# Macaron transformer layer: the additions to x of the last product but one, held behind the fifth chunk's operands in both feed-forwards

## The chip, the cores and the metric

The kernel runs on one core of a Trainium2 chip. The metric is the device time of one execution in microseconds (us). Five engines work in parallel and each takes its instructions strictly in the order of its queue: TensorE (PE, matrix products), VectorE (DVE, element-wise work), ScalarE (ACT, element-wise functions and copies), GpSimd (POOL, element-wise work here) and SyncE (SP, which issues the DMAs). An instruction that waits for another engine holds up everything behind it on its own engine.

## The reference

One layer on x of 1024 rows by 1024 columns: a feed-forward, a causal attention, a feed-forward.

```
x = x + 0.5 * swiglu(rms_norm(x, g1), w1_in, w1_out)
x = x + stick_breaking_attention(rms_norm(x, gm), w_qkv, gq, gk, w_o)
x = x + 0.5 * swiglu(rms_norm(x, g2), w2_in, w2_out)

def swiglu(xn, w_in, w_out):                 # w_in 1024 x 5632, w_out 2816 x 1024
    gate, up = split(xn @ w_in, 2)
    return (silu(gate) * up) @ w_out
```

All is float32. The edit is in the second matrix product of each feed-forward, `@ w_out`, and in the addition of its result to x.

## The kernel before, in words

**Products of three.** Each float32 operand is split in a high part and a low rest (function `split`, lines 182 and 183: ACT copies the high part, DVE or POOL subtracts it from the operand to get the low part). Each product is three matmuls (function `mm3`): high by high (line 279), high of the hidden values by low of the weights (line 280), low of the hidden values by high of the weights (line 281).

**The second product of a feed-forward** (function `ffn_out`) is done in blocks of 2 x 2 by Strassen's way: seven products instead of eight, numbered m = 1 to 7 and taken in the order 5, 1, 4, 3, 7, 2, 6 of the table `SEVEN`. Each product's operands are mixtures of blocks of the weights (mixed by DVE, line 524) and mixtures of blocks of the hidden values, which the feed-forward's first half left in DRAM. The inner length of each product comes in six chunks (numbered 0 to 5 in the code): five of two pieces and a sixth of one. For each chunk `operands` loads, mixes and splits: the hidden part's low half goes to DVE, but for chunks 1, 3 and 5 of product 6 to POOL; the weights' low half always goes to POOL. Each product sums up in four PSUM banks of 128 x 512, tags "ma" or "mb". The last product but one, m = 2, lies in the four "mb" banks, the last, m = 6, in the four "ma" banks.

The last product takes its first three chunks for all four banks (24 matmuls each), and then, bank by bank ("block 0" to "block 3"), the last three chunks (15 matmuls each), so that results come out one after another.

**Additions to x.** A finished bank is added to one or two quarters of x, which is in SBUF as two halves of 512 columns, tiles x0 and x1 (function `result`, line 570, DVE). Product 2 goes to both halves: eight additions of 128 x 512, two for each of its four banks. Product 6 goes to x1 alone: four additions, one behind each block.

**Holding.** `ffn_out` takes `held`. With `held=None` the eight additions of product 2 follow it at once in program order. With a number they are left until the last product's operands have been written down, and made to depend on chunk `held` of them:

```
there = ops[held][1][1][:, 0, 0:1].bitcast(F32)
signs = cpool.tile([P, 2], F32, name="signs")
dve.tensor_scalar(signs, there.to_broadcast([P, 2]), 1.0, None, op0=ALU.mult)
late_result(signs, ops)
```

`ops[held][1][1]` is the low half of that chunk's hidden operand. `signs` reads it (line 576), is then overwritten by two memsets with the factors +0.5 and -0.5 (line 536), and the additions take their factor from it. So none of them can start before that low half is there. The scheduler, which orders the instructions of each engine, sets the rest.

**What follows in the first feed-forward.** The hook `at` does, for product 2's half of x: squares of x0 with their sums (line 217, ACT, tile `hs`) and stores of x0 to `x_keep` (line 672, SP). For rows 6 and 7 of eight, whose x was ready earlier, it makes the normalised rows `xs` on DVE (line 242; the one-column writes of line 240 hold them behind the third chunk's low half). PE transposes them (line 254) into the "mb" banks behind block 0 of product 6, ACT and DVE split them into `xh` and `xl`. For the rows whose x is ready last DVE takes squares' sums to rates (lines 191 to 198) and normalises each block. The attention's first projection (`bq`, its weights `wqh` and `wql`) follows; its weights come by SP (`raw_qkv`, line 733) and are split by ACT (line 739) and POOL (line 742).

**In the second feed-forward** the hook only stores the output (line 1104, SP).

Before, the first feed-forward has `held=2`, the third chunk; the second has no `held`.

Of the kernel before, what the change touches and what calls it, by code (L numbers as in the profile page):

```python
# [9 lines left out]
F32 = mybir.dt.float32  # L10
# [7 lines left out]
P = 128  # L18
# [88 lines left out]
def macaron_kernel(ctx, tc, x, g1, w1_in, w1_out, gm, w_qkv, gq, gk, w_o, g2, w2_in, w2_out, out):  # L107
# [3 lines left out]
    cpool = ctx.enter_context(tc.tile_pool(name="cpool", bufs=1))  # L111
# [8 lines left out]
    @contextmanager  # L120
    def pools(*names, side=None):

        with ExitStack() as s:
            yield {n: s.enter_context(tc.tile_pool(name=n, bufs=2, side=side, reuse_waits="tile")) for n in names}
# [3 lines left out]
    @contextmanager  # L128
    def banks(name):

        with tc.tile_pool(name=name, bufs=1, space=PSUM, reuse_waits="tile") as p:
            psum.append((p, {}))
            yield
            psum.pop()
# [37 lines left out]
    make_identity(nc, ident)  # L172
    xh = cpool.tile([P, KD, T], F32R, name="xh")
    xl = cpool.tile([P, KD, T], F32R, name="xl")
    above = cpool.tile([P, 96], F32, name="above")
    pool_e.memset(below, 0.0)
    pool_e.memset(above, 0.0)
    x_keep = [dram.tile([T, D], F32, name=f"x_keep{i}") for i in range(2)]
# [22 lines left out]
    def load_gain(pl, g):  # L201

        t = pl["xs"].tile([P, D], F32, name="gain", bufs=1)
        sp.dma_start(t, g.broadcast_to([P, D]))
        return t
# [3 lines left out]
    def rows(tb):  # L209
        return slice(tb * P, (tb + 1) * P)  # L210
# [18 lines left out]
    def norm(pl, row, tbs, gain, ss=None, r=None, behind=None):  # L229

        if r is None:
            r = rates(pl, row, tbs, ss)
        turns = []
        for i, tb in enumerate(tbs):
            xs = pl["xs"].tile([P, D], F32, name="xs")
            if behind is not None:
                dve.tensor_scalar(xs[:, 0:1], behind, 1.0, None, op0=ALU.mult)  # L240
            for h in range(2):
                dve.scalar_tensor_tensor(
                    out=xs[:, HALVES[h]], in0=row(tb, h), scalar=r[:, i : i + 1], in1=gain[:, HALVES[h]],
                    op0=ALU.mult, op1=ALU.mult,
                )
            turns.append(partial(turned, xs, tb))
        return turns
# [35 lines left out]
    def mixed(pl):  # L283

        return [pl[f"tl{i}"].tile([P, 4, NHALF], F32, name=f"tl{i}", bufs=1) for i in range(4)]
# [10 lines left out]
    def stream(pl, w_in, q, part):  # L296

        c0 = part * F + q * 2 * P
        halves = []
        for d in range(2):  # L300
            raw = raw_tile(pl).rearrange("p (k c) -> p k c", k=4)
            sp.dma_start(
                raw, w_in[d * NHALF : (d + 1) * NHALF, c0 : c0 + 2 * P].rearrange("(k p) c -> p k c", p=P)
            )
            halves.append(raw)
        return halves
# [286 lines left out]
    def keeps(name):  # L593

        return {
            m: [dram.tile([P, len(qs), NHALF], F32, name=f"{name}_{m}_{c}") for c, qs in enumerate(CHUNKS)]
            for m in range(1, 8)
        }
# [17 lines left out]
    keep = keeps("k1")  # L616
    pending = []
    with pools(*RAWS) as pr:
        ops = {}
        right = ExitStack()  # L620
        tl = mixed(right.enter_context(pools(*MIXED, side="right")))
        with banks("ps1"), pools(*STREAM) as pa:
            with pools("x") as px, pools("xs", "hs", side="right") as pl:
                rows_of = {}

                def load_x(tbs):
                    for tb in tbs:
                        rows_of[tb] = px["x"].tile([P, D], F32, name="x", bufs=NT)
                        sp.dma_start(rows_of[tb], x[rows(tb), :])

                def normed(tbs):
                    pending.extend(norm(pl, lambda tb, h: rows_of[tb][:, HALVES[h]], tbs, gain))

                def turn_rows(tbs):
                    while pending:
                        pending.pop(0)("kb", tl)
                    if tbs:
                        normed(tbs)

                load_x(ORDER[:2])  # L640
                gain = load_gain(pl, g1)
                ahead = [stream(pr, w1_in, 0, 0)]
                load_x(ORDER[2:4])
                ahead.append(stream(pr, w1_in, 0, 1))
                load_x(ORDER[4:])
                for tb in ORDER[:2]:
                    normed((tb,))

                us = first_weights(pa | pr, ahead, pending[1].args[0][:, D - 1 :])
                turn_rows(ORDER[2:4])  # L650
                at = {(0, 3): 4, (1, 1): 6, (2, 1): 8}
                hb = first_pair(
                    pa | pr, us, {w: lambda i=i: turn_rows(ORDER[i : i + 2]) for w, i in at.items()}
                )
            with pools(*SPLIT) as pt:
                ffn_in(pa | pr | pt, w1_in, keep, tl, hb, right, lambda: early(pr, w1_out, keep, ops))
        late = []
        norms = ExitStack()
        pn = norms.enter_context(pools("xs", "hs", side="right"))
        with banks("ps2"), pools(*SECOND) as pl:  # L660
            lay_banks()
            gain_m = load_gain(pn, gm)
            half = pn["xs"].tile([P, 4, 2], F32, name="half", bufs=1)

            def at(x_sb, m, where, ops):
                def row(tb, h):
                    return x_sb[h][:, tb, :]

                def store(tbs, hs):
                    for tb in tbs:  # L670
                        for h in hs:
                            sp.dma_start(x_keep[0][rows(tb), HALVES[h]], row(tb, h))

                def turn_rows(bk, n):
                    for _ in range(n):
                        pending.pop(0)(bk)

                if (m, where) == (7, "end"):
                    pending.extend(norm(pn, row, (4, 5), gain_m))
                    store((4, 5, 6, 7), (0, 1))  # L680
                elif (m, where) == (2, 2):
                    turn_rows("ma", 2)
                elif (m, where) == (2, 3):
                    late.append(rates(pn, row, (6, 7)))
                elif (m, where) == (6, 0):

                    there = ops[2][1][1][:, 0, 0:1].bitcast(F32)
                    pending.extend(norm(pn, row, (6, 7), gain_m, r=late.pop(), behind=there))
                elif (m, where) == (2, "end"):
                    squares(pn, row, range(4), half, (0,))  # L690
                    store(range(4), (0,))
                elif m == 6 and str(where).startswith("block"):
                    t = int(where[-1])
                    turn_rows("mb", (2, 0, 0, 1)[t])
                    squares(pn, row, (t,), half[:, t : t + 1], (1,))
                    late.append(lambda: pending.extend(norm(pn, row, (t,), gain_m, half[:, t : t + 1])))
                    if t < 3:
                        late.pop()()
                    store((t,), (1,))

            ffn_out(pl | pr, w1_out, keep, x, ops, at, held=2)

    on_banks = ExitStack()
    on_banks.enter_context(banks("psa"))
# [3 lines left out]
    with ExitStack() as stack:  # L708
        pl = dict(stack.enter_context(pools(
            "raw_qkv", "wq1", "wq0", "wq2", "wq3", "vst0", "qk1", "qk0", "vst1", "st1", "st0", "sq",  # L710
        )))
# [247 lines left out]
        for p in range(-1, NP):  # L959
# [32 lines left out]
            if 0 <= p < NP - 2:  # L992

                held = (
                    ((dve, 0, lambda s=nxt: s["r"][:, 0, 0:1]), (pool_e, 1, lambda s=nxt: s["qk", 1][:, 0, 4, 0:1])),
                    ((pool_e, 0, lambda s=nxt: s["qk", 0][:, 2, 0, 0:1]),),
                )
# [21 lines left out]
    keep = keeps("k2")  # L1019
    after = ExitStack()  # L1020
    pr = after.enter_context(pools(*RAWS))
    pn = norms.enter_context(pools("xs", "hs", side="right"))
    with pools(*PROJECTION) as pl:
        pl = pl | pr | pn
# [60 lines left out]
    ops = {}  # L1085
# [5 lines left out]
    with banks("ps4"), pools(*SECOND) as pl:  # L1091
        lay_banks()

        def at(x_sb, m, where, ops):
            tbs, hs = (), ()
            if (m, where) == (7, "end"):
                tbs, hs = (4, 5, 6, 7), (0, 1)
            elif (m, where) == (2, "end"):
                tbs, hs = range(4), (0,)
            elif m == 6 and str(where).startswith("block"):  # L1100
                tbs, hs = (int(where[-1]),), (1,)
            for tb in tbs:
                for h in hs:
                    sp.dma_start(out[rows(tb), HALVES[h]], x_sb[h][:, tb, :])

        ffn_out(pl | pr, w2_out, keep, x_keep[1], ops, at)
    after.close()


# [37 lines left out]
```

## Time and profile before

| | |
|---|---|
| Runs | 1952.72 us median of 3 (1952.14 to 1958.2) |
| Profiled execution | 1957.07 us, its span 1955.3 us |
| PE busy | 1910.4 us, 98% of the span |
| DVE, ACT, POOL busy | 1265.6, 986.2, 1089.5 us |
| Mean granted clock of PE | 0.999 |
| End of the first feed-forward's last product | about 672 us |
| Last product of the second feed-forward | about 1916 to 1951.5 us |

A row of a timeline gives the start in us, the duration in us, engine, line and operation, what is written and read, a count, and in brackets how long the engine sat idle before and what released it. The matmuls of the profile overlap: one of 0.39 us starts every 0.227 us. `x`, `ma` or `raw` in the profile stand for all tiles of the name; the order's rows below have them with numbers.

### The profile page before, as it was taken

To read this page: it belongs to the slowest core of one execution; us is meant where nothing else is said; L and a number is where in the kernel's file an instruction comes from. 1 tells how busy PE (TensorE), PEld (TensorE's weight loads), DVE (VectorE), ACT (ScalarE), POOL (GpSimd) and SP (SyncE) were. 2 spreads that over 40 slices of the span, in tenths; PEclk is the share of its full clock that TensorE was granted. 3 is DMA by queue.
4 is the path that set the end of the run, shared out by engine and by line. 5 is a ranking of instruction groups with operands and counts; after the bars stand their busy time and mean duration, and the time that the engine had idled before them with its cause. 6 is when DMAs were issued, how large, how long until landed. Compare 5 with 4: busy or idle time off the path is not lost. (4 is left out here: it accounts for less than half of the span.)

```text
span 1955.3 us, 27335 instructions
## 1 busy us (share of the span) xinstructions
PE 1910.4 (98%) x9656; PEld 1638.2 (84%) x9656; DVE 1265.6 (65%) x1839; ACT 986.2 (50%) x1802; POOL 1089.5 (56%) x963
## 2 busy tenths in 40 slices
PE   7999999999999899999999999999999999999998
PEld 7978888888888798898989897789888888888886
DVE  7855545535766957877787878475555545557644
ACT  6533433434335467877787777344433443434331
POOL 3667666656455446555655664114667667655554
PEclk9999999999999999999999999999999999999999
DMA  6223223338996311011111144511323223369973
GB/s 210 85 88 126 101 92 114 107 113 284 343 325 231 124 34 44 31 46 45 36 34 46 55 130 151 194 55 44 130 86 124 96 99 105 117 231 345 325 251 128
DMA packets 168505, 260.26 MB, mean 133 GB/s; under 512 B 11568, under 2 KB 81200, under 8 KB 168368
## 3 DMA queue, kind: packets, MB, share of 16 engines
q1 hardware_dynamic: 168368, 258.52, 38.7%
q8 instruction: 75, 1.23, 0.3%
q14 instruction: 62, 0.51, 0.1%
HBM read 198.18 MB, written 60.29 MB: 132 GB/s over the span
## 5 line engine op out<-in xcount | busy, mean ns | idle before, releaser
L183 POOL TENSOR_TENSOR rp<-raw,rp 128x1024 fp32r<-128x1024 f32 x84 | 209.4, 2498 | 190.6 <-ACT rp L182 172.8
L183 POOL TENSOR_TENSOR u<-sf,u 128x512 fp32r<-128x512 f32 x160 | 225.9, 1414 | 151.1 <-ACT u L182 147.2
L183 POOL TENSOR_TENSOR u<-raw,u 128x512 fp32r<-128x512 f32 x136 | 195.8, 1444 | 164.7 <-ACT u L182 163.5
L182 ACT ACTIVATE u<-sf 128x512 fp32r<-128x512 f32 x160 | 100.7, 630 | 215.1 <-PE kb L280 86.7
L862 POOL TENSOR_TENSOR w<-w,om 128x512 f32<-128x512 f32 (+4 forms) x128 | 140.9, 1105 | 115.0 <-DVE om L855 88.8
L398 DVE TENSOR_TENSOR h<-h 128x512 f32<-128x512 f32 x110 | 135.4, 1235 | 85.7 <-POOL h L502 85.0
L279 PE MATMUL bq<-wqh,xh 128*128 128x384 f32 x512 | 174.7, 341 | 1.9 <-DVE vst L776 1.9
L182 ACT ACTIVATE rp<-rh 128x1024 fp32r<-128x1024 f32 (+1 forms) x78 | 76.4, 984 | 190.9 <-PE mb L280 62.0
L281 PE MATMUL bq<-wqh,xl 128*128 128x384 f32 x512 | 172.2, 336 | 0.0
L280 PE MATMUL bq<-wql,xh 128*128 128x384 f32 x512 | 172.1, 336 | 0.0
L279 PE MATMUL ka<-xh,u 128*128 128x512 f32 (+1 forms) x448 | 162.1, 362 | 1.8 <-ACT s L450 1.5
L280 PE MATMUL ka<-xl,u 128*128 128x512 f32 (+1 forms) x448 | 161.8, 361 | 0.0
L281 PE MATMUL ka<-xh,u 128*128 128x512 f32 (+1 forms) x448 | 161.6, 361 | 0.0
L182 ACT ACTIVATE u<-raw 128x512 fp32r<-128x512 f32 x136 | 85.0, 632 | 149.4 <-PE ka L280 101.3
L524 DVE TENSOR_TENSOR raw<-raw 128x1024 f32<-128x1024 f32 (+1 forms) x60 | 94.0, 1569 | 98.2 <-DMA raw<-w_out 92.4
L280 PE MATMUL ma<-rp 128*128 128x512 f32 x352 | 137.7, 391 | 4.4 <-POOL rp L183 4.4
L281 PE MATMUL ma<-rp 128*128 128x512 f32 x352 | 137.9, 392 | 3.3 <-DVE rp L183 3.3
L279 PE MATMUL ma<-rp 128*128 128x512 f32 x352 | 137.7, 391 | 0.0
L853 ACT ACTIVATE w<-bz,f 128x512 f32<-128x512 f32 (+2 forms) x192 | 112.3, 585 | 40.5 <-PE bz L849 39.4
L502 POOL TENSOR_TENSOR h<-h,g 128x512 f32<-128x512 f32 x80 | 112.9, 1411 | 35.2 <-DVE h L454 33.4
L427 DVE TENSOR_TENSOR sf<-raw 128x512 f32<-128x512 f32 x80 | 81.2, 1015 | 78.0 <-POOL u L183 78.0
L183 DVE TENSOR_TENSOR rp<-rh,rp 128x1024 fp32r<-128x1024 f32 (+1 forms) x70 | 108.4, 1567 | 22.4 <-ACT rp L182 19.7
(276 smaller groups left out, 5552.7 us busy)
## 6 DMA issues: line engine op xcount, KB each, us to landing
raw<-w_out SPq DMA_DIRECT2D x120, 512.0 KB, 5.6
raw<-w_in SPq DMA_DIRECT2D x88, 512.0 KB, 3.6
k<-h SPq DMA_DIRECT2D x154, 256.0 KB, 2.1
rh<-k SPq DMA_DIRECT2D x64, 512.0 KB, 6.2
raw_qkv<-w_qkv SPq DMA_DIRECT2D x64, 192.0 KB, 2.9
x_keep<-x SPq DMA_DIRECT2D x32, 256.0 KB, 3.5
x<-x_keep SPq DMA_DIRECT2D x32, 256.0 KB, 5.3
raw<-w_out SPq DMA_DIRECT2D x24, 256.0 KB, 4.3
```

Source lines behind the costliest of these rows:

```text
L182: act.activation(hi, raw, AF.Copy)
L183: (engine or dve).tensor_tensor(lo, raw, hi.bitcast(F32), op=ALU.subtract)
L279: pe.matmul(dst, ah, bh, start=start and i == 0, stop=False, skip_group_check=onto)
L280: pe.matmul(dst, ah, bl, start=False, stop=False, skip_group_check=onto)
L281: pe.matmul(dst, al, bh, start=False, stop=stop and i == n - 1, skip_group_check=onto)
L398: dve.tensor_tensor(src, hb[of[0]], hb[of[1]], op=getattr(ALU, of[2]))
L427: dve.tensor_tensor(f[n], x, y, op=op)
L502: pool_e.tensor_tensor(h, h, gs[k], op=ALU.mult)
L524: dve.tensor_tensor(w[0], w[0], w[1], op=getattr(ALU, W_OF[m][2]))
L853: act.activation(to, z, AF.Sigmoid, scale=state["f", half][:, sign, tb % 4, hd : hd + 1])
L862: pool_e.tensor_tensor(wt[:, c1 : c0 + n], wt[:, c1 : c0 + n], om[:, c1 - 1 : c0 + n - 1], op=ALU.mult)
```

## The change

Three numbers are edited. Both feed-forwards hold the eight additions of product 2 behind chunk 4, the fifth; so the second feed-forward, which held nothing, gets a `signs` tile of its own. The tile `above`, which is set to zero and not read, gives up eight columns (32 bytes of each partition).

```
-    above = cpool.tile([P, 96], F32, name="above")
+    above = cpool.tile([P, 88], F32, name="above")
...
-            ffn_out(pl | pr, w1_out, keep, x, ops, at, held=2)
+            ffn_out(pl | pr, w1_out, keep, x, ops, at, held=4)
...
-        ffn_out(pl | pr, w2_out, keep, x_keep[1], ops, at)
+        ffn_out(pl | pr, w2_out, keep, x_keep[1], ops, at, held=4)
```

PE's order stays. What moves on the other engines is at three places; the numbers behind names are those of single tiles.

DVE near the end of the second feed-forward, before. `raw_19325` is the fifth chunk's weights, `rp_19305` the third chunk's low half, `raw_19340` the sixth chunk's weights, `rp_19335` the fifth chunk's low half; `mb0` to `mb3` are the banks of product 2:

```order
L524 TENSOR_TENSOR raw_19325<-raw_19325,raw_19327 128x1024
L570 SCALAR_TENSOR_TENSOR x0_17887<-mb0_19041,x0_17887 128x512
L570 SCALAR_TENSOR_TENSOR x1_17888<-mb0_19041,x1_17888 128x512
L570 SCALAR_TENSOR_TENSOR x0_17887<-mb1_19042,x0_17887 128x512
L570 SCALAR_TENSOR_TENSOR x1_17888<-mb1_19042,x1_17888 128x512
L570 SCALAR_TENSOR_TENSOR x0_17887<-mb2_19043,x0_17887 128x512
L570 SCALAR_TENSOR_TENSOR x1_17888<-mb2_19043,x1_17888 128x512
L570 SCALAR_TENSOR_TENSOR x0_17887<-mb3_19044,x0_17887 128x512
L570 SCALAR_TENSOR_TENSOR x1_17888<-mb3_19044,x1_17888 128x512
L183 TENSOR_TENSOR rp_19305<-rh_19299,rp_19304 128x1024
L524 TENSOR_TENSOR raw_19340<-raw_19340,raw_19342 128x512
L183 TENSOR_TENSOR rp_19335<-rh_19329,rp_19334 128x1024
```

The same place of the changed kernel, where the tiles are `raw_19313`, `rp_19293`, `raw_19328` and `rp_19323`:

```order
L524 TENSOR_TENSOR raw_19313<-raw_19313,raw_19315 128x1024
L183 TENSOR_TENSOR rp_19293<-rh_19287,rp_19292 128x1024
L524 TENSOR_TENSOR raw_19328<-raw_19328,raw_19330 128x512
L183 TENSOR_TENSOR rp_19323<-rh_19317,rp_19322 128x1024
L576 TENSOR_SCALAR signs_19343<-rp_19323 128x2
L536 MEMSET signs_19343 128x1 x2
L570 SCALAR_TENSOR_TENSOR x0_17887<-mb0_19041,signs_19343,x0_17887 128x512
L570 SCALAR_TENSOR_TENSOR x1_17888<-mb0_19041,signs_19343,x1_17888 128x512
```

The eight additions (two are shown) have gone behind the third chunk's low half, the sixth chunk's mix and the fifth chunk's low half. On SP the sixth chunk's second load of weights, which stood behind the first store of the output, stands ahead of all stores.

DVE at the same place of the first feed-forward, before (`rp_5830` third chunk's low half, `raw_5865` sixth chunk's weights, `xs` normalised rows; the fifth chunk's low half comes behind seven of the additions, below these rows):

```order
L183 TENSOR_TENSOR rp_5830<-rh_5824,rp_5829 128x1024
L576 TENSOR_SCALAR signs_5880<-rp_5830 128x2
L240 TENSOR_SCALAR xs_5928<-rp_5830 128x1
L240 TENSOR_SCALAR xs_5932<-rp_5830 128x1
L536 MEMSET signs_5880 128x1 x2
L242 SCALAR_TENSOR_TENSOR xs_5928<-x0_4340,rs_y_5738,gain_4337 128x512
L570 SCALAR_TENSOR_TENSOR x0_4340<-mb0_5525,signs_5880,x0_4340 128x512
L570 SCALAR_TENSOR_TENSOR x1_4341<-mb0_5525,signs_5880,x1_4341 128x512
L524 TENSOR_TENSOR raw_5865<-raw_5865,raw_5867 128x512
```

And in the changed kernel (`rp_5860` fifth chunk's low half):

```order
L183 TENSOR_TENSOR rp_5830<-rh_5824,rp_5829 128x1024
L240 TENSOR_SCALAR xs_5928<-rp_5830 128x1
L240 TENSOR_SCALAR xs_5932<-rp_5830 128x1
L242 SCALAR_TENSOR_TENSOR xs_5932<-x1_4341,rs_y_5738,gain_4337 128x512
L242 SCALAR_TENSOR_TENSOR xs_5928<-x0_4340,rs_y_5738,gain_4337 128x512
L242 SCALAR_TENSOR_TENSOR xs_5932<-x0_4340,rs_y_5738,gain_4337 128x512
L524 TENSOR_TENSOR raw_5865<-raw_5865,raw_5867 128x512
L183 TENSOR_TENSOR rp_5860<-rh_5854,rp_5859 128x1024
L576 TENSOR_SCALAR signs_5880<-rp_5860 128x2
L536 MEMSET signs_5880 128x1 x2
L570 SCALAR_TENSOR_TENSOR x0_4340<-mb0_5525,signs_5880,x0_4340 128x512
```

The rest of the normalising, the sixth chunk's mix and the fifth chunk's low half have come ahead of the additions.

ACT at that place, before (`rp_5842` fourth chunk's weights; `rp_5859` and `rp_5857` fifth chunk's hidden part and weights; `rp_5874` and `rp_5872` those of the sixth; `hs` squares of x0):

```order
L182 ACTIVATE rp_5842<-raw_5835 128x1024
L217 ACTIVATE hs_5892,half_4339<-x0_4340 128x512
L217 ACTIVATE hs_5894,half_4339<-x0_4340 128x512
L182 ACTIVATE rp_5859<-rh_5854 128x1024
L182 ACTIVATE rp_5857<-raw_5850 128x1024
L217 ACTIVATE hs_5896,half_4339<-x0_4340 128x512
L217 ACTIVATE hs_5898,half_4339<-x0_4340 128x512
L182 ACTIVATE rp_5874<-rh_5869 128x512
L182 ACTIVATE rp_5872<-raw_5865 128x512
L739 ACTIVATE wqh_6232<-raw_qkv_6234 128x768
L739 ACTIVATE wqh_6232<-raw_qkv_6240 128x768
```

And in the changed kernel:

```order
L182 ACTIVATE rp_5842<-raw_5835 128x1024
L182 ACTIVATE rp_5859<-rh_5854 128x1024
L182 ACTIVATE rp_5857<-raw_5850 128x1024
L217 ACTIVATE hs_5892,half_4339<-x0_4340 128x512
L217 ACTIVATE hs_5894,half_4339<-x0_4340 128x512
L182 ACTIVATE rp_5874<-rh_5869 128x512
L182 ACTIVATE rp_5872<-raw_5865 128x512
L217 ACTIVATE hs_5896,half_4339<-x0_4340 128x512
L739 ACTIVATE wqh_6232<-raw_qkv_6234 128x768
L217 ACTIVATE hs_5898,half_4339<-x0_4340 128x512
L739 ACTIVATE wqh_6232<-raw_qkv_6240 128x768
```

The fifth chunk's two splits have gone ahead of the first two squares, the sixth chunk's from behind four squares to behind two. On SP the four stores of x0 (line 672) stood together ahead of the attention's weight loads (line 733); now loads and stores alternate: load, store, load, store, load, store, load, store, and four more loads.

## The prediction

> **What bounds the kernel now.** I read the page's header first, then the list of what TensorE (PE) waited for, then the timeline of each engine around the two places that the edit touches.
>
> ```profile
> span 1955.3 us, 27335 instructions
> PE 1910.4 (98%) x9656; PEld 1638.2 (84%) x9656; DVE 1265.6 (65%) x1839; ACT 986.2 (50%) x1802; POOL 1089.5 (56%) x963
> ...
> PE ma L280 <- POOL rp L183: 4.4, 2, 2.7
> PE ma L281 <- DVE rp L183: 3.3, 1, 3.3
> PE bq L279 <- DVE vst L776: 1.9, 2, 1.0
> ```
>
> PE is busy for 98% of the span, so only its waits are worth anything. The columns of the last three rows are total us, times, longest. The first two are waits inside the last product of a feed-forward: 4.4 us in two pieces in the first feed-forward, 3.3 us in one piece in the second. The third is a wait of the attention's first projections, just behind the first feed-forward, for VectorE (DVE). The edit concerns these three and no other.
>
> Second feed-forward, PE and then DVE, GpSimd (POOL), the DMA queue (SP):
>
> ```profile
> 1923.75 0.39 PE L279 MATMUL ma<-rp 128*128 128x512 f32 x1
> ...
> 1927.38 0.39 PE L280 MATMUL ma<-rp 128*128 128x512 f32 x1
> 1931.06 0.79 PE L281 MATMUL ma<-rp 128*128 128x512 f32 x1 [3.30 <-DVE rp L183]
> 1931.64 0.63 PE L279 MATMUL ma<-rp 128*128 128x512 f32 x1
> ...
> 1951.30 0.24 PE ma L281
> ...
> 1932.00:1933.00 1.00, 1.00 (x4) 0.74 (x3) 0.74 (x1) 0.34 (x1) 0.59 (x1) 0.50 0.00 0
> ```
>
> ```profile
> 1921.73 3.36 DVE L524 TENSOR_TENSOR raw<-raw 128x1024 f32<-128x1024 f32 x1 [2.34 <-POOL rp L183]
> 1925.01 4.86 DVE L570 SCALAR_TENSOR_TENSOR x<-mb,x 128x512 f32<-128x512 f32 x8
> 1929.80 1.21 DVE L183 TENSOR_TENSOR rp<-rh,rp 128x1024 fp32r<-128x1024 f32 x1
> 1930.93 0.68 DVE L524 TENSOR_TENSOR raw<-raw 128x512 f32<-128x512 f32 x1
> ...
> 1921.59 2.42 POOL L183 TENSOR_TENSOR rp<-raw,rp 128x1024 fp32r<-128x1024 f32 x1
> 1926.32 2.38 POOL L183 TENSOR_TENSOR rp<-raw,rp 128x1024 fp32r<-128x1024 f32 x1 [2.31 <-ACT rp L182]
> 1928.67 1.26 POOL L183 TENSOR_TENSOR rp<-rh,rp 128x512 fp32r<-128x512 f32 x1
> ...
> 1925.72 0.34 SPq L1104 DMA_DIRECT2D out<-x  x1
> 1926.15 0.38 SPq L319 DMA_DIRECT2D raw<-w_out  x1
> ```
>
> The row at 1929.80 is the low half of the third chunk's hidden operand, for which PE stops at 1927.38. It stands in DVE's queue behind the eight additions to x (1925.01, 4.86 us), which nobody needs yet. After the stall the granted clock is 0.50 (third column from the right of the stretch 1932 to 1933).
>
> First feed-forward, PE, ScalarE (ACT), DVE, POOL, SP:
>
> ```profile
> 653.02 0.40 PE L279 MATMUL ma<-rp 128*128 128x512 f32 x1
> 656.10 0.50 PE L280 MATMUL ma<-rp 128*128 128x512 f32 x1 [2.69 <-POOL rp L183]
> 657.36 0.39 PE L279 MATMUL ma<-rp 128*128 128x512 f32 x1
> 659.47 0.50 PE L280 MATMUL ma<-rp 128*128 128x512 f32 x1 [1.72 <-POOL rp L183]
> ...
> 648.17 0.63 ACT L217 ACTIVATE hs<-x 128x512 f32<-128x512 f32 x1 [5.61 <-DVE x L570]
> 650.78 1.05 ACT L182 ACTIVATE rp<-rh 128x1024 fp32r<-128x1024 f32 x1
> 653.42 0.63 ACT L217 ACTIVATE hs<-x 128x512 f32<-128x512 f32 x1
> 654.05 0.61 ACT L182 ACTIVATE rp<-rh 128x512 fp32r<-128x512 f32 x1
> 654.57 0.61 ACT L182 ACTIVATE rp<-raw 128x512 fp32r<-128x512 f32 x1
> 659.67 0.85 ACT L739 ACTIVATE wqh<-raw_qkv 128x768 fp32r<-128x768 f32 x1 [2.04 <-DMA raw_qkv<-w_qkv]
> 660.68 2.07 ACT L182 ACTIVATE xh<-mb 128x512 fp32r<-128x512 f32 x4 [0.17 <-PE mb L254]
> ...
> 635.19 2.89 DVE L242 SCALAR_TENSOR_TENSOR xs<-x,rs_y,gain 128x512 f32<-128x512 f32 x1
> 643.01 3.42 DVE L183 TENSOR_TENSOR rp<-rh,rp 128x1024 fp32r<-128x1024 f32 x1
> 646.47 0.17 DVE L576 TENSOR_SCALAR signs<-rp 128x2 f32<-128x2 f32 x1
> 646.73 0.75 DVE L242 SCALAR_TENSOR_TENSOR xs<-x,rs_y,gain 128x512 f32<-128x512 f32 x1
> 647.39 1.40 DVE L570 SCALAR_TENSOR_TENSOR x<-mb,signs,x 128x512 f32<-128x512 f32 x2
> 649.31 3.38 DVE L570 SCALAR_TENSOR_TENSOR x<-mb,signs,x 128x512 f32<-128x512 f32 x5
> ...
> 642.64 2.71 POOL L183 TENSOR_TENSOR rp<-raw,rp 128x1024 fp32r<-128x1024 f32 x1 [2.32 <-ACT rp L182]
> ...
> 648.17 4.87 SPq L672 DMA_DIRECT2D x_keep<-x  x4
> 656.65 0.62 SPq L733 DMA_DIRECT2D raw_qkv<-w_qkv  x1
> ```
>
> Here the additions are already held, behind the third chunk. ACT still waits: its squares of x (L217) sit ahead of the splits of the fifth chunk (650.78) and of the sixth (654.05), and POOL, which finishes those operands, is late for PE twice.
>
> **Second feed-forward: the gain.** The edit puts the eight additions behind the fifth chunk's low half. The third chunk's low half then follows the mix at 1921.73 and runs from 1925.0 to 1926.2 (1.21), before POOL's next operation (1926.32). PE wants it at 1927.6. The stall of 1931.06 - 1927.38 - 0.227 = 3.45 us goes; 0.227 is the pitch of matmuls, 16 intervals from 1923.75 to 1927.38. So does the slow clock: from the matmul at 1931.06 to the last one (1951.30) are 81 intervals (22 left of the third chunk, 60 of the four blocks), 18.38 us at 0.227, and the rows give 20.24. That is 1.86 us more, 5.31 in all.
>
> What is late next: after 1926.2 the sixth chunk's mix (0.68) ends at 1926.9; POOL's 2.38 then runs to 1929.2; the fifth chunk's low half, overlapping it, waits and ends at about 1930.4. PE needs that at 1933.9 and the sixth chunk's weights, POOL's last work, at 1935.3; they are ready by about 1933.4. The eight additions run from about 1932 to 1937.5, of which only the first block's own addition (1936.0) is delayed, by 1.5 us, with three blocks (10 us) behind it. The multiplier in memory instead of an immediate (about 0.07 us each), the one signs instruction and two memsets lie in this slack: nothing. On SP the sixth chunk's weights stood behind the first store of the output (1925.72, 1926.15) and now go ahead of it, soon after the third chunk's POOL work frees their buffer; the stores go later but still before the last block. If this load delays the one ahead of it, the mix at 1921.73 has slack: it is not through before POOL's operation ends (1921.59 + 2.42). The tail behind the last matmul stays. Bounds: -5.31 when the stall and the slow clock both go, -3.45 if the clock would have stayed full anyway, 0 if another operand holds PE as long. I take -5.3, as the rows have both.
>
> **First feed-forward: the stall moves.** The additions go from behind the third chunk to behind the fifth. On DVE come first three normalising operations (L242), the sixth chunk's mix and the fifth's low half; on ACT the fifth chunk's splits now precede the first two squares, but the sixth chunk's splits stay behind them. Worked out:
> - DVE ends the third chunk's low half at 646.4 as now. POOL's weights of the fifth chunk, no longer waiting for ACT, start there. An SBUF operation of DVE that overlaps one of POOL takes about as long as both (643.01: 3.42 beside POOL's 642.64, against 1.21), so DVE's first L242 gets through only after POOL's 2.4, at 649.5, the other two at 650.9, the mix at 651.5, the low half at 652.7. PE wants it at 653.5: the first stall goes.
> - 0.25 us later (from 646.47 to 647.39 less one L242 at 0.67) the first addition starts, 652.95, and they follow every 0.676 us (3.38 / 5). The third starts at 654.3. ACT's second square starts 0.78 behind it (648.17 against 647.39), 655.1; the sixth chunk's splits 0.63 and 1.15 later (654.05, 654.57 against 653.42), the last ending at 656.9. POOL then takes 1.26 twice (1928.67, beside the eight additions of the second feed-forward) from 656.3: 658.9. PE would be at this chunk at 653.02 + 6 x 0.227 = 654.4, so it waits there for 4.5 us, with one matmul inside. Now it gets past at 659.47: 0.55 us gained.
> - That is no gain for the attention. ACT turns rows into xh (660.68) only after two weight splits (L739), the second of which (659.67) starts 3.0 us after its load's issue (656.65). On SP the loads now alternate with the stores of x: this load follows the third store, which follows the fifth addition (ends 652.95 + 4 x 0.676 + 0.74 = 656.4) by 0.6: issue at 657.0, split at 660.0 to 660.85, xh at 660.85. That is 0.17 later. DVE's norms follow xh, and the attention's projections wait for DVE (1.9 us in the waits).
>
> So the first feed-forward gives 0.2 us back. Its bounds: -4.7, the two stalls measured start to start (3.08 + 2.11, less 2 x 0.227), if ACT's squares held nothing; and +1.9, if the longer wait costs the clock that the second one cost. I take +0.2.
>
> The Trainium skill, "TensorE: Matmul & The Clock Gate", Part 1, says that the clock halves after an idle window of some 3.4 us which runs free of the program, and comes back after as long a busy one. The trace agrees in that 3.30 us idle was followed by 0.50 and 2.69 us was not. By that rule the drop is a matter of phase in each run: the 1.86 us may be absent from some runs of before (the sum is then -3.45 + 0.2 = -3.2), and the wait of 4.5 us, longer than a window, may bring one to the first feed-forward.
>
> **Sum.** -5.3 + 0.2 = -5.1 us against the profiled execution's own 1957.07 (span 1955.3 and 1.8 around it): 1952.0. That execution is 4.3 us above the median of the runs, 1952.72; I carry the difference over: 1947.6.
>
> **Rivals.**
> 1. Both feed-forwards gain. If DVE's additions started early enough for ACT's squares, the sixth chunk would be in time: -5.3 - 4.7 = -10.0, 1942.7. For it: PE's waits there are all for operands. Against it: the order of ACT, and the projections' wait for DVE, which stays.
> 2. The clock's part comes out otherwise: either the unprofiled runs of before lacked the drop (-3.2, 1949.5), or the first feed-forward gains a drop of up to 1.9 (-5.1 + 1.7 = -3.4, 1949.3), or both (1951.2). For it: 4.5 us is longer than the 3.30 that led to 0.50.
> 3. The second feed-forward stalls as long elsewhere, for the fifth or sixth chunk's operands: +0.2, 1952.9. Against it: over 1.9 us of slack for each.
> 4. Slower. DVE's chain ahead of the held additions in the first feed-forward collides with POOL at each step: three L242 at 2.89 instead of 0.67 and the low half at 3.42 instead of 1.21 make 8.9 us more, of which the estimate has 2.4 already. All behind it (squares, sixth chunk, stores, weight loads, xh) moves by 6.5, the attention with it: -5.1 + 6.5 = +1.4, 1954.1, and with a drop of the clock (1.9) 1956.0. It turns the whole slower once the first addition starts after 652.95 + 5.1 = 658.1. Against it: POOL has one operation to do in that stretch.
>
> **Chances.** As forecast (1946 to 1949): 0.55; rival 1: 0.10; rival 2: 0.20; rival 3: 0.10; rival 4: 0.05. A change of 0.3%, 5.9 us, is about what a measurement of this kernel can tell from none. The forecast of -5.1 lies just inside it; I give over a third of its chance, with rival 1, to faster: 0.30. Slower by as much is rival 4 with the spread of the runs of before (1952.14 to 1958.2) on top, or a case that I have not seen: 0.05. The rest, 0.65, is within the bound. The range runs from between the forecast and rival 1, 1943.5, to just above rival 3, 1953.5.
>
> **What would show it.** In the second feed-forward: no PE wait at line 281, a granted clock of 1.0 to the end, the eight additions at about 1932 of the old time. In the first: no wait at the fifth chunk, one at the sixth of about 4 us with ACT's splits behind the second square, the first addition at about 653, xh from the transposes at about 661. Wrong would be: a PE wait in the second feed-forward, a sixth chunk ready in time in the first, or an attention that starts more than 1 us earlier or later than now.

## The result and the profile after

| | before | after |
|---|---|---|
| Runs | 1953.1 us median of 4 (1952.14 to 1958.2) | 1967.72 us median of 4 (1966.6 to 1968.37) |
| Profiled execution | 1957.07 us, span 1955.3 | 1967.79 us, span 1965.7 |
| Ratio of the runs | | 1.0069, 95% interval 1.0051 to 1.0087 |

The changed kernel is slower, by 0.7%, and its time lies 14 us above the upper end of the predicted range. The page of after, header and busy times, then rows of the list of PE's waits (total us, times, longest):

```profile
span 1965.7 us, 27341 instructions
PE 1927.1 (98%) x9656; PEld 1636.7 (83%) x9656; DVE 1259.7 (64%) x1842; ACT 987.5 (50%) x1802; POOL 1088.5 (55%) x963
...
PE bq L279 <- DVE vst L776: 1.9, 2, 1.0
PE ma L279 <- ACT rp L182: 1.6, 1, 1.6
PE ma L280 <- POOL rp L183: 1.6, 1, 1.6
```

The wait at line 281 is gone and the two at line 280 have shrunk from 4.4 us to 3.2 (1.6 of it at line 279). Yet PE is busy for 16.7 us more with the same 9656 matmuls: the matmuls themselves take longer. The groups of PE's instructions, shapes kept apart (line, engine, what is written and read, shape, count; then busy us and mean ns of one), before:

```profile
L279 PE MATMUL ka<-xh,u 128*128 128x512 f32 x320 | 124.6, 389 | 1.5 <-ACT s L450 1.5
L279 PE MATMUL ka<-t1h,u 128*128 128x512 f32 x160 | 62.2, 389 | 0.0
L281 PE MATMUL mb<-rp 128*128 128x512 f32 x264 | 102.7, 389 | 0.0
```

and after:

```profile
L279 PE MATMUL ka<-xh,u 128*128 128x512 f32 x320 | 126.8, 396 | 0.1
L279 PE MATMUL ka<-t1h,u 128*128 128x512 f32 x160 | 63.3, 395 | 0.0
L281 PE MATMUL mb<-rp 128*128 128x512 f32 x264 | 102.8, 389 | 0.0
```

The slower groups are those of the first halves of the feed-forwards (`ka`, `kb`, `kc`), which the change was not about. They take weights from tiles `u` and have `xh` or `xl`, or blocks mixed from these (`t0h`, `t1h`, ...), as the moving operand. The second halves (`rp`) are as before. Since a row's duration overlaps the next matmul, the pitch shows it better. PE alone in a stretch of the first feed-forward's first half, busy us and (x matmuls), granted clock, share of the DMA engines, GB/s; before, then after:

```profile
300.00:400.00 100.00, 100.00 (x443) 1.00 0.34 114
```

```profile
300.00:400.00 100.00, 100.00 (x432) 1.00 0.31 106
```

443 matmuls in 100 us before, 432 after, both at a granted clock of 1.00 and with no wait. Matching the n-th matmul of one trace with the n-th of the other, after's lag behind before grows like this:

| Place | lag, us |
|---|---|
| first feed-forward, end of the first half | 7.3 |
| behind its last product | 7.9 |
| attention, end | 7.8 |
| second feed-forward, end of the first half | 15.6 |
| at the matmul that ends before's stall in the last product | 12.2 |
| last matmul | 10.5 |

So the second feed-forward's last product gained 5.2 us, as forecast, and the first halves lost 7.3 and 7.8 us. By the starts of the matmuls the mean pitch of those of 128 x 512 in the first halves is 231.9 ns instead of 226.7; 1680 of them in each make 8.8 us. Two things take some of it back: in the first feed-forward a wait of 1.5 us for ACT's `s` has shrunk to 0.1 (the last column of the `xh` groups above), and the smaller matmuls of 128 x 256 with which each first half begins became a little faster, 116.7 ns instead of 120.0 in the second feed-forward (384 of them: 0.9 us less). The only part of the edit that reaches the first halves is the one of which the prediction says nothing: `above`, from 96 columns to 88. Behind it in SBUF lie all other tiles of the left side, among them the weights `u`; they have moved by 32 bytes against `xh` and `xl`, which lie ahead of it. (Places in SBUF, here and below, are those of the built programs; a profile does not show them.)

### The profile page after: what moved, and what is told of

The parts are those of the page before. It is cut to its first block, busy times and chain, and to the rows that moved or that the text cites. A ratio compares the mean times of both kernels' runs of the same rounds, so it can differ in the third digit from the quotient of the medians.

```text
span 1965.7 us, 27341 instructions
## 1 busy us (share of the span) xinstructions
PE 1927.1 (98%) x9656; PEld 1636.7 (83%) x9656; DVE 1259.7 (64%) x1842; ACT 987.5 (50%) x1802; POOL 1088.5 (55%) x963
## 4 chain that ended last, share of the span: by engine, by line
PE 83%; DVE 8%; issue 3%; ACT 2%; DMA 2%; POOL 2%; SPq 0%; DVEq 0%; ACTq 0%; POOLq 0%
PE ka L279 6%; PE ka L281 6%; PE ka L280 6%; PE kc L279 4%; PE kc L281 4%; PE kc L280 4%; PE kb L279 4%; PE kb L281 4%; PE kb L280 4%; PE bq L279 4%; PE bq L280 3%; PE bq L281 3%; PE ma L280 3%; PE ma L279 3%; PE ma L281 3%; PE bo L902 3%
## 5 line engine op out<-in xcount | busy, mean ns | idle before, releaser
L183 POOL TENSOR_TENSOR u<-sf,u 128x512 fp32r<-128x512 f32 x160 | 232.0, 1452 | 138.2 <-ACT u L182 134.2
L183 POOL TENSOR_TENSOR rp<-raw,rp 128x1024 fp32r<-128x1024 f32 x84 | 204.7, 2440 | 186.0 <-ACT rp L182 172.6
```

What stands on the lines that cost most here:

```text
L183: (engine or dve).tensor_tensor(lo, raw, hi.bitcast(F32), op=ALU.subtract)
```

## The experiments

**1. The parts apart.** Four kernels, the kernel before with one or two of the three edits each.

`pad88_only`: `above` alone.

```
-    above = cpool.tile([P, 96], F32, name="above")
+    above = cpool.tile([P, 88], F32, name="above")
```

> The kernel before with the tile above cut from 96 to 88 columns and no hold changed. Theory A (the move of all later tiles by 32 bytes slows the matmuls of the first halves of the feed-forwards): their pitch goes from 226.7 to about 231.9 ns in both, 1680 matmuls each, so about 15 to 16 us slower than before, near 1968.5; both stalls of the last products stay as before. Theory B (the holds themselves slow the kernel, by the order of instructions that they give): the pitch stays at 226.7 ns and the time at 1953.

Measured: 1971.76 us (1967.01 to 1975.76), against 1953.33 of before; ratio 1.0087 (1.0066 to 1.0107). A row of PE's waits and the stretch of above, in its profile:

```profile
PE ma L281 <- DVE rp L183: 4.7, 1, 4.7
```

```profile
300.00:400.00 100.00, 100.00 (x432) 1.00 0.31 106
```

The whole loss comes from eight columns of a tile that nothing reads; and without the holds the stall at line 281 is still there. Counted from the first matmul, the last one lags 17.2 us behind that of before's first profile. Of these 15.5 have come by the end of the second feed-forward's first half, as expected; the rest comes at that stall, which is 1.4 us longer here, and behind it.

`holds_only`: both holds, `above` as before.

```
+            ffn_out(pl | pr, w1_out, keep, x, ops, at, held=4)
...
+        ffn_out(pl | pr, w2_out, keep, x_keep[1], ops, at, held=4)
```

> Both feed-forwards held behind the fifth chunk, above left at 96 columns. Theory A: pitch 226.7 ns in the first halves as before, the stall of 3.3 us in the second feed-forward gone, the first feed-forward unchanged within 0.5 us: 5 us faster than before, about 1948. Theory B: as slow as the changed kernel, about 1967.

Measured: 1952.53 us (1951.32 to 1953.39), ratio 0.9986 (0.9976 to 0.9995). The median is below those of both kernels, but only 0.14% below the one of before; the 5 us that were expected did not come. The second `signs` tile needed no room of its own: it is placed where the first one was.

`hold_second`: the second feed-forward's hold alone.

```
+        ffn_out(pl | pr, w2_out, keep, x_keep[1], ops, at, held=4)
```

> Only the second feed-forward held behind the fifth chunk, the first left at the third, above at 96. Theory A with the prediction's term of the second feed-forward: no PE wait in its last product and a granted clock of 1.0 to the end, 3.5 to 5.3 us faster than before, about 1948. Theory B: slower than before if it is this hold that costs.

Measured: 1952.74 us (1951.92 to 1954.59), ratio 0.9995 (0.9986 to 1.0003). Its last matmul comes 4.8 us earlier than that of before's first profile. DVE near the end of the second feed-forward:

```profile
1923.26 2.19 DVE L524 TENSOR_TENSOR raw<-raw 128x1024 f32<-128x1024 f32 x1 [3.50 <-DMA raw<-w_out]
1925.38 1.21 DVE L183 TENSOR_TENSOR rp<-rh,rp 128x1024 fp32r<-128x1024 f32 x1
...
1930.57 1.15 DVE L576 TENSOR_SCALAR signs<-rp 128x2 f32<-128x2 f32 x1
...
1931.88 0.75 DVE L570 SCALAR_TENSOR_TENSOR x<-mb,signs,x 128x512 f32<-128x512 f32 x1
```

The third chunk's low half (1925.38) is through before PE's 1927.6 and the first addition starts at 1931.88. The stall is gone, but the median of the runs has hardly moved.

`hold_first`: the first feed-forward's hold alone.

```
+            ffn_out(pl | pr, w1_out, keep, x, ops, at, held=4)
```

> Only the first feed-forward held behind the fifth chunk, the second without a hold, above at 96. Theory A with the prediction's term of the first feed-forward: within 0.5 us of before (plus 0.2), up to 1.9 us slower if the clock drops; the wait at the fifth chunk gone, one for the sixth chunk in its place. Theory B: slower than before by several us if it is this hold that costs.

Measured: 1956.66 us (1951.75 to 1959.08), ratio 1.0005 (0.9993 to 1.0016). The median says little, because the runs lie in two groups: 7 of 12 are at 1955.9 or more, the others at 1954.0 or less. So do the 29 runs of before taken beside these four kernels: 16 at 1953.5 or less, 13 at 1956.8 or more. All 23 runs of the two kernels with the second hold are at 1954.6 or less. The second hold acts on the upper group alone. A median hides this, a mean shows it: 1954.8 for before, 1952.9 for `hold_second`, 1952.4 for `holds_only`. Before's 13 of 29 runs in the upper group, at 5.2 us each, are 2.3 us of such a mean.

**2. Why before has two groups.** `before_again` is the kernel before with nothing edited, profiled a second time.

> The kernel before itself, profiled once more, since its timed runs lie in two groups near 1952.4 and 1957.6 and its first profile (1957.07) is of the upper one. Theory P: the groups differ by whether the fifth chunk's mix on DVE in the second feed-forward gets through before POOL's work on the fourth chunk's weights (in the first profile it started 0.14 us behind it and took 3.36 us) - a run near 1952.4 then shows this mix at 1.2 us and a PE wait of under 1 us in the last product instead of 3.3. Theory C: the groups differ by the halved clock behind that stall alone - a run of the lower group shows the wait of 3.3 us and no slow window, and would be near 1955. A run near 1957 repeats the first profile and tells nothing new.

Measured: 1952.11 us, span 1950.0. The execution falls in the lower group, and PE has no wait at line 281 at all. The traces agree within 0.4 us up to the last stretch and part there. DVE, POOL and SP in this execution of the lower group:

```profile
1887.77 1.37 DVE L524 TENSOR_TENSOR raw<-raw 128x1024 f32<-128x1024 f32 x1 [12.76 <-DMA raw<-w_out]
...
1917.53 1.53 DVE L524 TENSOR_TENSOR raw<-raw 128x1024 f32<-128x1024 f32 x1 [2.56 <-DMA raw<-w_out]
1918.98 4.86 DVE L570 SCALAR_TENSOR_TENSOR x<-mb,x 128x512 f32<-128x512 f32 x8
1923.77 3.44 DVE L183 TENSOR_TENSOR rp<-rh,rp 128x1024 fp32r<-128x1024 f32 x1
...
1888.33 3.08 POOL L183 TENSOR_TENSOR rp<-raw,rp 128x1024 fp32r<-128x1024 f32 x1 [0.27 <-ACT rp L182]
...
1889.17 0.38 SPq L319 DMA_DIRECT2D raw<-w_out  x1
```

and in the first profile of before, of the upper group:

```profile
1888.58 3.30 DVE L524 TENSOR_TENSOR raw<-raw 128x1024 f32<-128x1024 f32 x1 [13.49 <-DMA raw<-w_out]
...
1888.41 2.39 POOL L183 TENSOR_TENSOR rp<-raw,rp 128x1024 fp32r<-128x1024 f32 x1 [0.27 <-ACT rp L182]
...
1891.90 0.38 SPq L319 DMA_DIRECT2D raw<-w_out  x1
```

A mix on DVE (line 524) waits for a DMA. Where the transfer lands early, the mix starts 0.56 us ahead of POOL's operation and takes 1.37 us. Where it lands 0.81 us later, it starts 0.17 us behind POOL's and takes 3.30 us. The Trainium skill, "SBUF — State Buffer", section "SBUF: two separate sides", says that DVE and GpSimd share one pair of ports, which whoever starts first holds for the whole instruction; these rows agree, with 1.37 against 3.30 us. The next load of weights waits for that mix, so SP issues it 2.73 us later (1891.90 against 1889.17), and the delay grows to 4.2 us at the fifth chunk's mix (1921.73 in the prediction's rows, 1917.53 here). In the lower group the eight additions are over by 1923.8 and the low half behind them by 1927.2, just in time for PE. From the stall on, the lower group gains 5.2 us on the upper one, exactly what the second hold gains there.

These rows are of two executions, but the other traces agree. Of the ten executions traced without the second hold, five have the stall at line 281; in these five the mix at about 1888 us starts 0.17 to 0.31 us behind POOL's operation, in the other five 0.23 to 0.67 us ahead of it. In `hold_second` and in after it comes late too (0.22 and 0.17 us behind), and there is no stall. Why the transfer lands early or late is not known.

**3. What about the move makes the matmuls slow.** Tiles behind `above` are moved by other distances, or together with `xh` and `xl`.

`pad112`:

```
-    above = cpool.tile([P, 96], F32, name="above")
+    above = cpool.tile([P, 112], F32, name="above")
```

> The kernel before with above at 112 columns: all later tiles 64 bytes further on. If the pitch of the first halves' matmuls goes by the place of the weight tiles modulo 64 bytes (0 in the kernel before, 32 in the changed one), it stays at 226.7 ns and the time at 1952 to 1958. If any move of the later tiles against xh and xl, which stay, slows them, it is at 230 ns or more and the time at 1967 or more.

Measured: 1966.38 us. The same stretch of PE:

```profile
300.00:400.00 100.00, 100.00 (x434) 1.00 0.32 110
```

So more room is as bad as less.

`below24`: the tile ahead of `xh` larger, so that all moves together.

```
-    below = cpool.tile([P, 16], F32, name="below")
+    below = cpool.tile([P, 24], F32, name="below")
```

> The kernel before with the tile below at 24 columns instead of 16: xh, xl and all later tiles 32 bytes further on together, so that nothing moves against anything else on this side. If the place modulo 64 bytes counts, the first halves are slow (231 to 234 ns, 1967 or more). If the distance between the tiles counts, they stay at 226.7 ns.

Measured: 1958.31 us, an execution of the upper group (it has the wait of 3.3 us at line 281).

```profile
300.00:400.00 100.00, 100.00 (x443) 1.00 0.34 116
```

The pitch is that of before, with `xh`, `xl` and every tile behind them 32 bytes off their old places.

`below24_above88`: `xh` and `xl` moved by 32 bytes, the weights back at their old place.

```
+    below = cpool.tile([P, 24], F32, name="below")
...
+    above = cpool.tile([P, 88], F32, name="above")
```

> The kernel before with below at 24 and above at 88 columns: xh and xl 32 bytes further on, everything behind them where it was. If the place of the weight tiles (u) counts, which stay at a multiple of 64, the pitch stays at 226.7 ns. If that of the moving operand xh and xl counts, the products with xh are slow and those with the mixed tiles t are not. If their distance counts, it is as slow as in the changed kernel for xh.

Measured: 1969.24 us.

```profile
300.00:400.00 100.00, 100.00 (x433) 1.00 0.32 108
```

Slow again. What counts is where the tiles lie against each other, not where they lie.

`pad128` and `pad160`: `above` at 128 and at 160 columns, a distance of 128 and of 256 bytes more.

```
+    above = cpool.tile([P, 128], F32, name="above")
```

> The kernel before with the tile `above` at 128 columns in place of 96: the weights and everything behind it lie 128 bytes further from the halves of x, nothing else is changed. Moves of 32 and 64 bytes made the matmuls with x as the moving operand take 395 to 396 ns in place of 389 and the run 14 to 16 us longer. Theory A1 (what counts is the distance modulo 128 bytes or less): 389 ns, and 1952 or 1957 us. Theory A2 (modulo 256 or 512 bytes): 395 ns or more, and 1965 to 1970 us.

```
+    above = cpool.tile([P, 160], F32, name="above")
```

> The kernel before with `above` at 160 columns: the weights lie 256 bytes further from the halves of x. Theories A1 and a modulus of 256 bytes: 389 ns and 1952 or 1957 us. A modulus of 512 bytes: 395 ns or more and 1965 to 1970 us.

Measured: 1971.81 us and 1953.32 us. The stretch in `pad128`, then in `pad160`:

```profile
300.00:400.00 100.00, 100.00 (x435) 1.00 0.32 111
```

```profile
300.00:400.00 100.00, 100.00 (x443) 1.00 0.34 115
```

A move of 128 bytes is slow, one of 256 is not: of the moves tried (32, 64, 128 and 256 bytes), only that of 256 bytes leaves the pitch as it was.

`half_u`: which tile is the partner. A tile of 8 columns that nothing reads is placed ahead of the weight tiles u8 to u15 and one of 56 columns behind them: these eight of eighteen weight tiles lie 32 bytes off modulo 256 against everything else.

```
-        *(f"u{i}" for i in range(8, 16)), *(f"h{i}" ...
+        "gap8", *(f"u{i}" for i in range(8, 16)), "gap56", *(f"h{i}" ...
...
+            pl[f"gap{n}"].tile([P, n], F32, name=f"gap{n}", bufs=1)
```

> The kernel before with a gap of 32 bytes ahead of the weight tiles u8 to u15 of the first halves of the feed-forwards, and one of 224 bytes behind them, so that these eight of the eighteen weight tiles alone lie otherwise, by 32 bytes, and all behind them lie 256 bytes further, which pad160 showed to be no change. `above` stays at 96. Theory B1 (what counts is where the weights of a matmul lie against its moving operand): matmuls whose weights are in u8 to u15 become slower, with x and now also with t0, t1, t3 as the moving operand, those with the other ten tiles stay at a pitch of 226.7 ns; 8/18 of 16 us, about 7 us longer. Theory B2 (x against some other tile behind it, such as those that other engines write at the time): no product is slower, 1952 or 1957 us.

Measured: 1968.05 us, with the stretch of PE

```profile
300.00:400.00 100.00, 100.00 (x437) 1.00 0.32 111
```

between the two. By products of twelve matmuls, with the place of their weights, from the starts of the matmuls from 250 us on (moving operand, start of the high weights' tile in bytes, mean pitch in ns):

```
x   130496  226.7        x   142784  227.0
t1  134592  226.7        t1  126400  226.7
x   138688  227.3        x   130496  226.7
x    93408  232.8        x   134592  226.7
t3   97504  233.3        t3  138688  227.4
x   101600  233.3        x    93408  232.8
t0  105696  233.4        ...
```

Just the products whose weights lie in u8 to u15 (93408 to 105696) are slow, whatever the moving operand is. Here `t0` to `t3` too have been moved against those weights, and they slow down as `x` does. The expected loss of about 7 us is there, 3.5 us in the first half of the first feed-forward and 4.6 in that of the second; the rest of this execution's 16 us is one wait of 6.3 us for weights at the start of the second feed-forward and the slow clock behind it. POOL's order differs there: the split that PE waits for has moved behind other work and starts only at 1320.5 us.

So theory B1 stands: a 128 x 512 matmul of these products is about 3% slower (233.3 ns instead of 226.7) when its weights and its moving operand do not start at the same place modulo 256 bytes. In before all of `xh`, `xl`, `t0h` to `t3l`, `u` and `rp` start at 192 modulo 256.

## Why the prediction was wrong, point by point

**The edit of `above`: the step that failed.** The prediction starts from "only its waits are worth anything" and says that the edit concerns three of PE's waits "and no other". So it took the time of the matmuls themselves as fixed, goes through the two holds, and gives the tile `above` neither a cost nor a bound. That step failed: with `above` edited the 128 x 512 matmuls of the first halves started every 231.9 ns instead of every 226.7, with no new wait. It cost 7.3 and 7.8 us, three times all that the rest gained. Nothing in the rows that were quoted could have given the price, but the step needed a sentence: every later tile moves by 32 bytes, 1920 matmuls of 128 x 512 read tiles on both sides of the move (the groups with `xh` or `xl` and `u`, of 320, 160 and 160 matmuls at each of three lines), and one nanosecond on each is 1.9 us. A bound from that would have opened the range upwards. No rival covered it either; rival 4, the one on the slower side, has another mechanism.

**The difference carried to the median.** -5.1 was worked out on an execution of 1957.07 and carried to a median of 1952.72. The runs lie in two groups, and that execution was of the upper one. In the lower group there is no stall to remove. So even without `above` the forecast of 1947.6 would have been missed: `holds_only` came to 1952.53, inside the range, but near rival 3's 1952.9 and for another reason than rival 3's. The prediction saw that an execution may lack the slow clock, and did not ask whether it may lack the stall. The timed runs shown (1952.14 to 1958.2) held a hint: their spread of 6 us is about the size of the stall and its slow clock.

**The second feed-forward, -5.31: right.** Measured start to start, it is -5.17 in after, in `hold_second` and in `holds_only`. There is no wait at line 281, and the granted clock is 1.00 to the end. This holds against an execution of the upper group, like the one that the forecast was worked out on. DVE in after, which lags behind the old time by 15.6 us here:

```profile
1939.03 1.69 DVE L524 TENSOR_TENSOR raw<-raw 128x1024 f32<-128x1024 f32 x1 [4.00 <-DMA raw<-w_out]
1940.64 1.21 DVE L183 TENSOR_TENSOR rp<-rh,rp 128x1024 fp32r<-128x1024 f32 x1
...
1942.38 3.43 DVE L183 TENSOR_TENSOR rp<-rh,rp 128x1024 fp32r<-128x1024 f32 x1
...
1947.14 5.36 DVE L570 SCALAR_TENSOR_TENSOR x<-mb,signs,x 128x512 f32<-128x512 f32 x8
```

The third chunk's low half follows the fifth chunk's mix in 1.21 us; the fifth chunk's overlaps POOL and takes 3.43; the additions start at 1947.14 - 15.6 = 1931.5, where about 1932 was forecast.

**The first feed-forward, +0.2: about right in the sum, partly by luck.** DVE, ACT, POOL and PE in after, 7.5 us later than the old time:

```profile
651.41 6.10 DVE L242 SCALAR_TENSOR_TENSOR xs<-x,rs_y,gain 128x512 f32<-128x512 f32 x3
...
659.61 5.36 DVE L570 SCALAR_TENSOR_TENSOR x<-mb,signs,x 128x512 f32<-128x512 f32 x8
...
661.77 0.63 ACT L217 ACTIVATE hs<-x 128x512 f32<-128x512 f32 x1 [0.65 <-DVE x L570]
...
662.92 0.61 ACT L182 ACTIVATE rp<-raw 128x512 fp32r<-128x512 f32 x1
...
668.01 1.59 ACT L182 ACTIVATE xh<-mb 128x512 fp32r<-128x512 f32 x3
...
650.15 6.15 POOL L183 TENSOR_TENSOR rp<-raw,rp 128x1024 fp32r<-128x1024 f32 x2 [2.32 <-ACT rp L182]
...
663.59 0.49 PE L279 MATMUL ma<-rp 128*128 128x512 f32 x1 [1.58 <-ACT rp L182]
665.66 0.50 PE L280 MATMUL ma<-rp 128*128 128x512 f32 x1 [1.57 <-POOL rp L183]
...
666.00:668.00 2.00, 2.00 (x11) 1.90 (x10) 0.69 (x1) 0.74 (x1) 1.65 (x2) 0.56 0.57 198
```

- The first addition starts at 659.61 - 7.5 = 652.1 (forecast 652.95), `xh` at 660.5 (660.85). DVE's three normalising operations do collide with POOL, 6.10 us for three, as rival 4 feared; but the later addition never came near its 658.1.
- The stall moved to the sixth chunk: two waits of 1.58 and 1.57 us with one matmul between. From start to start that is 665.66 - 661.62 - 0.227 = 3.8 us lost, where 4.5 was forecast, also with one matmul inside.
- Behind them the granted clock is 0.56. This is rival 2's drop in the first feed-forward, and it followed the two waits of 1.6 us, each shorter than the 2.69 that went without a drop in before. `pad160`, whose wait there is 2.60 us, has the drop too:

```profile
656.32 0.50 PE L280 MATMUL ma<-rp 128*128 128x512 f32 x1 [2.60 <-POOL rp L183]
```

  So the length of a wait does not decide it. The Trainium skill, "TensorE: Matmul & The Clock Gate", Part 1, says that the windows by which the clock goes run free of the program, so that it matters where in a window a wait falls. The traces agree: in each of them the changes of the granted clock lie whole multiples of 3.413 us apart. Here are the stretches of that length around the two waits, counted from the drops at 657.16 in `pad160` and at 1931.10 in before (PE's busy us and matmuls, granted clock, share of the DMA engines, GB/s), `pad160` first, then before:

```profile
653.74:657.16 3.42, 0.84 (x4) 1.00 0.62 192
657.16:660.57 3.41, 2.28 (x6) 0.50 0.40 115
```

```profile
651.11:654.52 3.41, 2.30 (x11) 1.00 0.58 210
654.52:657.94 3.42, 1.65 (x6) 1.00 0.51 145
657.94:661.35 3.41, 1.88 (x14) 1.00 0.32 91
```

  The 2.60 us fall in one stretch, PE is busy in it for 0.84 us, and the next stretch has half the clock. The 2.69 us are divided over two, with 2.30 and 1.65 us busy, and no drop follows. In after both waits fall in one (662.84 to 666.25, 1.09 us busy). So a stretch need not be wholly idle to be followed by a drop.
- In sum after's lag is 7.5 us ahead of these waits and 6.2 behind them: a gain of 1.3 where 0.55 was forecast. The slow clock, which the sum left out, then takes 1.7, so that the lag is 7.9 behind the product. In the attention, some 20 us later, it is 7.5 again. Against before, `hold_first` costs 0.9 us behind the product and 0.3 at that later place, `holds_only` 0.8 and 0.6; `before_again`, with nothing edited, differs from before's first profile by 0.4 there. So all lie within the bounds of -4.7 to +1.9, and +0.2 is as near as can be told, but by two errors that offset each other. The gain of rival 1 did not come.

## What to carry to other kernels

Cost every line of a diff, the one that only changes a tile's size too: ask what it moves in memory and which hot loop reads tiles on both sides of the move. When the timed runs spread by as much as the stall that is to go, look first whether the lower runs have that stall at all; only one profile's execution was seen. A change that bundles a gain and an unseen cost is best taken apart before it is dropped: here the part without the resize has a lower median than both kernels. And kernels whose runs lie in two groups are not to be compared by one profile each.

## What the runs showed of the hardware

- The pitch of matmuls of 128 x 512 with weights of 128 x 128 depended on where the moving operand and the weights lie against each other: 226.7 ns at before's distance and with 256 bytes more, about 233 with 32 bytes less or with 32, 64 or 128 more, at a granted clock of 1.00 in all. The Trainium skill, "SBUF — State Buffer", section "Who interferes with whom", gives TensorE two independent read ports, one for the moving operand and one for the weight load; by that no such dependence would be expected, and the measurement decides. What in the reading causes it is open. It is also open why products with `t0`, `t1` and `t3` in after, whose place against their weights had not changed, were slow for about the first seven of twelve matmuls when they followed one with x.
- The attention's first projections (128 x 384), where the weights `wqh` are the moving operand and `xh` is on the other side, had the same 32 bytes' move in after and took 342 ns instead of 341: hardly any effect. Matmuls of 128 x 256 with `xh` or `xl` and `u` went the other way, from 120.0 to 116.7 ns. So the loss was measured for one shape and is no rule for all.
- The granted clock was halved for whole stretches of 3.41 us, on a grid that stays the same through an execution. In the thirteen traces, from the first full clock on, every stretch of this grid in which PE was busy for up to 42% by the profile was followed by half clock, and none with over 52%; between these figures both occurred.
- A difference of 0.8 us in the landing of one transfer, through a DVE operation that comes behind POOL's instead of ahead of it, decided 5.2 us of the whole time.
